# Hybrid encoder on one core: the filters' loads on ScalarE's queue, c loaded onto every partition, the softplus in the first mixer

## The chip, the core and the metric

The kernel runs on one core of a Trainium2 chip. Its engines work from queues of their own and meet through semaphores: TensorE (PE, with its weight loads PEld), VectorE (DVE), ScalarE (ACT), GpSimd (POOL) and SyncE (SP). SP computes nothing; it issues DMA transfers, and ScalarE issues some too. The metric is the device time of one execution in microseconds; lower is better. The time before is the median of three runs.

## The reference

A two-layer encoder on 256 tokens of width 2048. Each layer is modulated by a vector c, and its mixer has four groups (a gated linear recurrence, attention, a Hyena long convolution with learned filters, an mLSTM), followed by a SwiGLU. What matters here, cut down:

```python
c_act = silu(c)
for l in range(2):
    mod = c_act @ ada_w[l] + ada_b[l]            # 6 x 2048 numbers for each layer
    sh1, sc1, g1, sh2, sc2, g2 = split(mod, 6)
    h = rmsnorm(x, norm_mix_g[l]) * (1 + sc1) + sh1
    proj = h @ w_in[l] + b_in[l]
    y = concat(rglru(...), attention(...), hyena(...), mlstm(...))
    x = x + g1 * (y @ w_out[l])
    x = x + g2 * swiglu(rmsnorm(x, norm_ffn_g[l]) * (1 + sc2) + sh2)
return rmsnorm(x, final_g)

# Hyena's filters, they depend on weights alone
h = sin(sf * (feat @ w1 + b1)); h = sin(sf * (h @ w2 + b2)); h = h @ w3
h = h * exp(-t * abs(decay)); h = h / norm(h); spectrum = rfft(two_sided(h))
# rglru, in its gates
log_a = -8 * softplus(-lam) * r
```

## The kernel before, in words

The sequence lies along the free dimension: `x` is 16 tiles of 128 x 256, one for each 128 channels. Matrix products take weights as `raw` tiles of 128 x 1024 (512 KB), split by ScalarE into `hi` (L343) and by VectorE into `lo` (L344), and multiply them with `h` (L387 for the first eight `h` unsplit, L390 to L394 for the others).

`mod = c_act @ ada_w` runs on VectorE: each block of 128 outputs is two halves, each a transfer of 512 KB (`ada` or `ad`, L455 or by `load`, L313/L316) and one multiply with accumulation (L474) against `cb`, silu(c) on all partitions. Layer 0 needs 64 such halves before its last normalised `h` can be made, and the first seven fill all buffers (three `ada`, four `ad`). The others can be loaded only as VectorE frees a buffer.

The start of the program, `run`, does these things: `filters` (two small products and sines for each layer, the sine's argument reduced by six VectorE operations, L582 to L587); `ada_init` (loads c as one row, takes silu, spreads it to 128 partitions by four matmuls with a row of ones, L428, and copies them to `cb`, L430); the load and squares of `x` (ScalarE, summed on GpSimd, L523), which give `rb`, the reciprocal root mean square; `spectra` (L607 onwards: `third` loads the filters' last weights `w3`, `dft` the five transform tiles; decay `dec` L647, filter values L651, `he` L653/L654, transforms L675, results written to memory by ScalarE's queue, L693), in which a loop calls `early`, which does two halves of `mod` a turn and makes the `h` they allow; then `softplus` (two ScalarE functions and 22 VectorE operations of 128 x 16 or 128 x 8).

The order in which the code is written is not the order on the engines. The program is built by a scheduler (`schedule_with_timeline_sim`) that lists each engine's instructions by its own estimate of time; on the chip each engine then takes them strictly in that order. All transfers take turns at eight completion semaphores, DMAHW0 to DMAHW7, whichever queue issues them; a transfer waits until the one that last held its semaphore has landed, so no more than eight are under way. Names in the trace: `w` is a tile of `w3` or of the filters' weights, `m` a bank of PSUM, `z` and `n` the sine's argument, `sx`, `sz`, `ss` and `lam` the softplus.

Of the kernel before, what the change touches and what calls it, by code (L numbers as in the profile page):

```python
# [13 lines left out]
AF = mybir.ActivationFunctionType  # L14
# [4 lines left out]
P = 128  # L19
# [229 lines left out]
class Net:  # L249
# [170 lines left out]
    def ada_init(self, order):  # L420
        nc = self.nc
        self.cb = self.cp.tile([P, D], F32, name="cb")
        row = self.cb[0:1, :]
        nc.sync.dma_start(row, self.d["c"])
        nc.scalar.activation(row, row, AF.Silu)
        ps = [self.bank("cb") for _ in range(4)]
        for i in range(4):
            nc.tensor.matmul(ps[i], self.misc[0:1, 0:1].to_broadcast([1, P]), row[:, i * 512:(i + 1) * 512], start=True, stop=True)  # L428
        for i in range(4):
            nc.scalar.activation(self.cb[:, i * 512:(i + 1) * 512], ps[i], AF.Copy)  # L430
        self.mod = [self.cp.tile([P, 96], F32, name=f"mod{l}") for l in range(DEPTH)]
        self.acc = [self.cp.tile([P, 96, 2], F32, name=f"acc{l}") for l in range(DEPTH)]

        self.gain = {(l, j): self.cp.tile([P, 16], F32, name=f"gain{l}{j}") for l in range(DEPTH) for j in (1, 4)}
        self.ada_items = [(l, b, h) for l, b in order for h in range(2)]
        self.ada_at = self.ada_got = 0
        self.ada_left = 0.0
        self.ada_tiles = {}
# [127 lines left out]
    def dft(self):  # L566
        k = []
        for i in range(5):
            t = self.slot("dft")
            self.load(t, self.d["k_dft"][:, i])  # L570
            k.append(t)
        return k
# [19 lines left out]
    def filters(self):  # L592
# [3 lines left out]
        nc.sync.dma_start(ft[:17, :], d["k_feat"])  # L596
        w = self.cp.tile([64, DEPTH, P], F32, name="hw")
        nc.sync.dma_start(w, d["hy_w"])
# [8 lines left out]
    def spectra(self, h):  # L607

        nc = self.nc
        w3 = self.third(0)  # L610
        self.kept_dft = dft = self.dft()
# [10 lines left out]
    def third(self, l):  # L622

        w3 = [self.slot("w3") for _ in range(4)]
        for q in range(4):
            self.nc.sync.dma_start(w3[q][:68, :], self.d["hy_w3"][l, q])
# [497 lines left out]
    def mixer(self, l, h):  # L1124
# [4 lines left out]
        for hf in range(2):  # L1129
# [4 lines left out]
            yc += self.hyena(l, hf, pv, dft, spec, self.rs[l])  # L1134
        px = self.proj(l, h, 12, 2)
# [83 lines left out]
    def run(self, out):  # L1219
        nc, d = self.nc, self.d  # L1220
        order = [(0, j * 16 + k) for k in range(16) for j in (1, 0)]
        order += [(l, j * 16 + k) for l in range(DEPTH) for j in ((1, 0) if l else ()) + (2, 4, 3, 5) for k in range(16)]
        h2 = self.filters()
        self.ada_init(order)
# [13 lines left out]
        self.softplus()  # L1238
# [27 lines left out]
```

## Time and profile before

| | us |
|---|---|
| median of three runs | 2565.73 |
| lowest and highest | 2561.16, 2567.45 |
| the profiled execution | 2563.17 |
| its span, first to last instruction | 2561.4 |

Around the span lie 1.8 us. Read the busy shares of the engines first, then the same shares by slices, then stretches of the start, and in them what each engine waits for. In a timeline row the first number is the start in us, the second the length of the merged instructions, then engine, line, operation, names, shapes and count; in square brackets how long the engine sat idle before, and what ended that. A q behind the engine (SPq, ACTq) marks its queue, where a transfer is issued.

### The profile page before, as it was taken

The page shows a single profiled execution, that of the slowest core. Times are in us where ns is not written, and L with a number is a line of the kernel's source. Part 1 is how long each engine was busy: PE and PEld are TensorE (multiplying, and loading weights), DVE is VectorE, ACT ScalarE, POOL GpSimd, SP SyncE. Part 2 cuts the span into 40 slices and gives each one's busy share as a digit, 9 for nine tenths or more (in the row PEclk, how much of TensorE's full clock was granted, in tenths as well). Part 3 has the DMA queues.
Part 4 walks back from the last instruction along what each step waited for, and adds up shares of the span by engine and source line. Part 5 has one row for each costly group of instructions (what it writes and reads, how often), then busy time and mean ns, then how long its engine had stood idle before and what let it go on. Part 6 is the DMA issues. An engine that isn't in the chain of part 4 may idle for free. (4 is left out here: it accounts for less than half of the span.)

```text
span 2561.4 us, 38913 instructions
## 1 busy us (share of the span) xinstructions
PE 2470.3 (96%) x14962; PEld 2164.6 (85%) x14962; DVE 1839.4 (72%) x2862; ACT 1160.4 (45%) x1788; POOL 151.6 (6%) x142
## 2 busy tenths in 40 slices
PE   6879999999999999999998998999999999999998
PEld 2459988898888888888888998979888888888887
DVE  6877667689777777877787768777755555555555
ACT  4423344544544444444444455554444344434443
POOL 2101110021000000000010101002000000000001
PEclk9999999999999999999999999999999999999999
DMA  7887787688888888888887767658655655665554
GB/s 269 318 320 257 269 279 257 203 316 286 294 286 287 294 288 292 284 297 290 281 289 258 250 220 242 221 166 281 228 194 185 189 192 189 184 188 192 188 179 132
DMA packets 180719, 629.63 MB, mean 246 GB/s; under 512 B 20162, under 2 KB 20371, under 8 KB 180531
## 3 DMA queue, kind: packets, MB, share of 16 engines
q1 hardware_dynamic: 130996, 453.05, 53.9%
q10 hardware_dynamic: 49536, 174.09, 19.3%
q8 instruction: 117, 1.92, 0.3%
q14 instruction: 70, 0.57, 0.1%
HBM read 618.67 MB, written 8.39 MB: 245 GB/s over the span
## 5 line engine op out<-in xcount | busy, mean ns | idle before, releaser
L344 DVE TENSOR_TENSOR lo<-raw,hi 128x1024 fp32r<-128x1024 f32 (+2 forms) x737 | 891.8, 1211 | 471.8 <-ACT hi L343 463.4
L343 ACT ACTIVATE hi<-raw 128x1024 fp32r<-128x1024 f32 (+2 forms) x737 | 765.9, 1041 | 943.9 <-PE a L390 404.9
L394 PE MATMUL a<-h,lo 128*128 128x256 f32 x3848 | 1070.1, 284 | 5.7 <-DVE lo L344 5.7
L390 PE MATMUL a<-h,hi 128*128 128x512 f32 x2624 | 909.6, 396 | 0.0
L394 PEld LDWEIGHTS a<-h,lo 128*128 128x128 f32 x3848 | 735.2, 191 | 21.9 <-DVE lo L344 6.3
L390 PEld LDWEIGHTS a<-h,hi 128*128 128x128 f32 x2624 | 483.7, 188 | 107.4
L390 PE MATMUL a<-g,hi 128*128 128x512 f32 x1352 | 463.0, 396 | 0.0
L474 DVE SCALAR_TENSOR_TENSOR ada<-ada,cb 128x1024 f32<-128x1024 f32 x342 | 426.6, 1250 | 36.7 <-DMA ada<-in_ada 36.3
L392 PE MATMUL a<-h,hi 128*128 128x256 f32 x1224 | 359.9, 297 | 17.4 <-ACT h L558 12.3
L394 PE MATMUL a<-g,lo 128*128 128x256 f32 x1408 | 368.9, 279 | 0.0
L393 PE MATMUL a<-h,hi 128*128 128x256 f32 x1224 | 359.2, 294 | 7.3 <-DVE h L560 7.3
L390 PEld LDWEIGHTS a<-g,hi 128*128 128x128 f32 x1352 | 243.0, 188 | 47.8
L394 PEld LDWEIGHTS a<-g,lo 128*128 128x128 f32 x1408 | 265.6, 189 | 13.2
L392 PEld LDWEIGHTS a<-h,hi 128*128 128x128 f32 x1224 | 239.8, 197 | 24.6 <-ACT h L558 14.5
L393 PEld LDWEIGHTS a<-h,hi 128*128 128x128 f32 x1224 | 241.1, 197 | 12.7 <-DVE h L560 8.4
L523 POOL TENSOR_TENSOR sq<-sq,sq 128x256 f32<-128x256 f32 x65 | 75.5, 1161 | 1654.5 <-issue 1365.1
L387 PE MATMUL a<-h,raw 128*128 128x256 f32 x688 | 165.4, 393 | 3.8 <-DMA raw<-in_w_in 3.2
L387 PEld LDWEIGHTS a<-h,raw 128*128 128x128 f32 x688 | 132.2, 197 | 32.6 <-issue 8.6
L1160 DVE SCALAR_TENSOR_TENSOR x<-a,mod,x 128x256 f32<-128x256 f32 x228 | 100.2, 476 | 28.0 <-PE a L394 28.0
L1177 ACT ACTIVATE s<-a 128x256 f32<-128x256 f32 x82 | 31.5, 384 | 119.1 <-PE a L394 119.1
L1178 DVE TENSOR_TENSOR s<-s,a 128x256 f32<-128x256 f32 x82 | 34.4, 420 | 35.9 <-ACT s L1177 35.9
L558 ACT ACTIVATE h<-h,mod 128x256 fp32r<-128x256 f32 (+1 forms) x64 | 29.5, 501 | 62.8 <-DVE h L554 36.4
(268 smaller groups left out, 2170.5 us busy)
## 6 DMA issues: line engine op xcount, KB each, us to landing
raw<-in_w SPq DMA_DIRECT2D x496, 512.0 KB, 4.6
ada<-in_ada ACTq DMA_DIRECT2D x320, 512.0 KB, 5.4
raw<-in_w_in SPq DMA_DIRECT2D x168, 512.0 KB, 5.3
raw<-in_w_out SPq DMA_DIRECT2D x64, 512.0 KB, 5.6
ad<-in_ada SPq DMA_DIRECT2D x42, 512.0 KB, 7.2
raw<-in_w SPq DMA_DIRECT2D x32, 384.0 KB, 3.7
ada<-in_ada SPq DMA_DIRECT2D x22, 512.0 KB, 6.1
spectra<-sl ACTq DMA_DIRECT2D x24, 256.0 KB, 7.4
```

Of the source, the lines that this page charges most:

```text
L343: self.hi_at = self.nc.scalar.activation(hi[:, :n], t[:, :n], AF.Copy).ins
L344: self.lo_at = self.nc.vector.tensor_tensor(lo[:, :n], t[:, :n], hi[:, :n].bitcast(F32), ALU.subtract).ins
L387: mm(o, hi[:, c], a[:, :T], start=first and b == 0, stop=last, skip_group_check=True)
L390: mm(ps[b], hi[:, c], a, start=first, stop=False, skip_group_check=True)
L392: mm(o, hi[:, c], a[:, :T], start=first and b == 0, stop=False, skip_group_check=True)
L393: mm(o, hi[:, c], a[:, T:], start=False, stop=False, skip_group_check=True)
L394: mm(o, lo[:, c], a[:, :T], start=False, stop=last, skip_group_check=True)
L474: nc.vector.scalar_tensor_tensor(t, t, 1.0, self.cb[:, h * 1024:(h + 1) * 1024], ALU.mult, ALU.mult, accum_out=acc[:, b, h:h + 1])
L523: nc.gpsimd.tensor_tensor(self.sq, self.sq, t, ALU.add)
L1160: i = self.nc.vector.scalar_tensor_tensor(self.x[k], o, g, self.x[k], ALU.mult, ALU.add)
L1177: nc.scalar.activation(s, ps[0][:, T:], AF.Copy)
L1178: nc.vector.tensor_tensor(s, s, ps[0][:, :T], ALU.add)
```

## The change

Four things are changed. c is loaded by one transfer onto all 128 partitions and silu taken there; the row, the four matmuls and the four copies go. The filters' features `feat`, their weights `hw`, the first layer's four `w3` tiles and the five transform tiles `dft` are loaded by ScalarE's queue, and `w3` and `dft` are asked for right after `filters` in place of inside `spectra`. `ada_init` stands ahead of `filters`. `softplus` is written in the first mixer, behind the two Hyena halves.

```diff
     def ada_init(self, order):
         self.cb = self.cp.tile([P, D], F32, name="cb")
-        row = self.cb[0:1, :]
-        nc.sync.dma_start(row, self.d["c"])
-        nc.scalar.activation(row, row, AF.Silu)
-        ps = [self.bank("cb") for _ in range(4)]
-        for i in range(4):
-            nc.tensor.matmul(ps[i], self.misc[0:1, 0:1].to_broadcast([1, P]), row[:, i * 512:(i + 1) * 512], start=True, stop=True)
-        for i in range(4):
-            nc.scalar.activation(self.cb[:, i * 512:(i + 1) * 512], ps[i], AF.Copy)
+        nc.sync.dma_start(self.cb, self.d["c"].to_broadcast([P, D]))
+        nc.scalar.activation(self.cb, self.cb, AF.Silu)
...
-    def dft(self):
+    def dft(self, first=False):
...
-            self.load(t, self.d["k_dft"][:, i])
+            if first:
+                self.nc.scalar.dma_start(t, self.d["k_dft"][:, i])
+            else:
+                self.load(t, self.d["k_dft"][:, i])
...
-        nc.sync.dma_start(ft[:17, :], d["k_feat"])
+        nc.scalar.dma_start(ft[:17, :], d["k_feat"])
-        nc.sync.dma_start(w, d["hy_w"])
+        nc.scalar.dma_start(w, d["hy_w"])
...
-        w3 = self.third(0)
-        self.kept_dft = dft = self.dft()
+        w3 = self.w3
+        self.kept_dft = dft = self.first_dft
...
-            self.nc.sync.dma_start(w3[q][:68, :], self.d["hy_w3"][l, q])
+            (self.nc.sync if l else self.nc.scalar).dma_start(w3[q][:68, :], self.d["hy_w3"][l, q])
...
+        if l == 0:
+            self.softplus()
         px = self.proj(l, h, 12, 2)
...
+        self.ada_init(order)
         h2 = self.filters()
-        self.ada_init(order)
+        self.w3 = self.third(0)
+        self.first_dft = self.dft(True)
...
-        self.softplus()
```

What the scheduler makes of it. SP's queue before, from the last of the first seven halves of `mod` to the eighth, `ada_246` (in brackets the semaphores an instruction waits for):

```order
L313 DMA ada_220<-in_ada 128x1024 [waits DMAHW0_49]
L626 DMA w_59_269<-in_hy_w 68x512 [waits DMAHW1_49]
...
L313 DMA dft_278<-in_k_dft 128x512 [waits DMAHW5_49]
...
L313 DMA dft_286<-in_k_dft 128x512 [waits DMAHW1_49]
L626 DMA w_118_429<-in_hy_w 68x512 [waits DMAHW2_49]
...
L328 DMA raw_455<-in_w_in 128x1024 [waits DMAHW6_49]
...
L328 DMA raw_465<-in_w_in 128x1024 [waits DMAHW3_49]
L313 DMA ada_246<-in_ada 128x1024 [waits DMAHW4_49,DVE_49]
```

The same place now; the eighth half is `ada_253`:

```order
L313 DMA ada_227<-in_ada 128x1024 [waits DMAHW1_49]
L623 DMA w_114_417<-in_hy_w 68x512 [waits DMAHW2_49]
...
L623 DMA w_117_420<-in_hy_w 68x512 [waits DMAHW5_49]
L328 DMA raw_443<-in_w_in 128x1024 [waits DMAHW6_49]
...
L328 DMA raw_453<-in_w_in 128x1024 [waits DMAHW3_49]
L313 DMA ada_253<-in_ada 128x1024 [waits DMAHW4_49,DVE_49]
```

Nineteen transfers stood between the two halves, of which ten are left; the four first `w` and the five `dft` have gone to ScalarE's queue.

ScalarE's queue at the start of the program, before:

```order
L1017 ACT_TABLE_LOAD
L1017 ACTIVATE sx<-lam 128x16 [waits DVE_49]
L1018 ACTIVATE sx<-sx 128x16 [waits Activation_49]
L425 ACT_TABLE_LOAD
L425 ACTIVATE cb<-cb 1x2048 [waits DMAHW5_49]
L517 ACTIVATE sq_162<-x 128x256 [waits DMAHW6_49]
```

and now:

```order
L593 DMA feat_93<-in_k_feat 17x256
...
L623 DMA w_21_148<-in_hy_w 68x512 [waits DMAHW3_49]
L625 ACT_TABLE_LOAD
L625 ACTIVATE w_18_145<-w_18_145 4x512 [waits DMAHW5_49]
...
L424 ACT_TABLE_LOAD
L424 ACTIVATE cb<-cb 128x2048 [waits DMAHW6_49]
L586 ACTIVATE sin_107<-z_99 64x256 [waits DVE_49]
...
L1015 ACT_TABLE_LOAD
L1015 ACTIVATE sx<-sx 128x16 [waits Activation_49]
...
L586 ACT_TABLE_LOAD [waits DVE_49]
```

Six issues stand first, and the first sine and the squares stand behind two waits for transfers; the softplus's second function (L1015) is still in the first rows, between the squares, and brings a change of table with it and one back. Four table loads stand here, of two before.

VectorE's queue up to the eighth half, before (`ada_207` is the first half):

```order
L587 TENSOR_SCALAR z_124<-z_124 64x256 [waits DVE_49]
L474 SCALAR_TENSOR_TENSOR ada_207,acc_151<-ada_207,cb 128x1024 [waits DMAHW2_49,Activation_49]
...
L654 TENSOR_TENSOR he_335<-m_333,he_335 128x512 [waits PE_49]
L474 SCALAR_TENSOR_TENSOR ada_246,acc_151<-ada_246,cb 128x1024 [waits DMAHW4_49]
L474 SCALAR_TENSOR_TENSOR ad_225,acc_151<-ad_225,cb 128x1024 [waits DMAHW5_49]
L481 SCALAR_TENSOR_TENSOR mod_149<-acc_151,par 128x1 [waits DVE_49]
L654 TENSOR_TENSOR he_366<-m_364,he_366 128x512 [waits PE_49,Activation_49]
```

and now (`ada_214` is the first half):

```order
L1017 TENSOR_SCALAR sz<-sx 128x16 [waits Activation_49]
L584 TENSOR_SCALAR z_123<-z_123 64x256 [waits DVE_49]
...
L468 SCALAR_TENSOR_TENSOR ada_214,acc_87<-ada_214,cb 128x1024 [waits DMAHW0_49]
L1023 TENSOR_TENSOR ss<-ss,sz_1730 128x16 [waits DVE_49]
...
L651 TENSOR_TENSOR he_323<-m_321,he_323 128x512 [waits PE_49]
L468 SCALAR_TENSOR_TENSOR ada_253,acc_87<-ada_253,cb 128x1024 [waits DMAHW4_49]
...
L468 SCALAR_TENSOR_TENSOR ad_256,acc_87<-ad_256,cb 128x1024 [waits DMAHW0_49]
L651 TENSOR_TENSOR he_354<-m_352,he_354 128x512 [waits PE_49,Activation_49]
```

The softplus starts later and reaches in between the first halves; five halves of `mod` (`ada_253`, `ad_232`, `ad_235`, `ada_264`, `ad_256`) now stand between `he_323` and `he_354`, where two stood between `he_335` and `he_366`.

## Rows read from the trace of the kernel before

**Rows 1.** The page: busy time of PE, and PE in 40 slices (tenths).

```profile
PE 2470.3 (96%) x14962; PEld 2164.6 (85%) x14962; DVE 1839.4 (72%) x2862; ACT 1160.4 (45%) x1788; POOL 151.6 (6%) x142
...
PE   6879999999999999999998998999999999999998
```

**Rows 2.** Stretches: us, busy us of PE, PEld, DVE, ACT, POOL, clock, DMA share, GB/s.

```profile
0.00:21.25 21.25, 10.31 (x16) 3.79 (x16) 16.59 (x52) 12.34 (x26) 10.26 (x17) 1.00 0.87 312
21.25:29.34 8.09, 3.61 (x14) 2.63 (x12) 8.09 (x16) 2.11 (x4) 0.00 (x0) 1.00 0.59 165
29.34:49.81 20.47, 16.21 (x23) 6.80 (x24) 4.24 (x13) 6.50 (x10) 1.60 (x2) 1.00 0.97 324
49.81:191.60 141.79, 120.39 (x417) 73.20 (x416) 116.87 (x232) 50.74 (x103) 19.23 (x12) 0.94 0.84 306
...
200.00:300.00 100.00, 100.00 (x592) 91.92 (x591) 74.43 (x124) 29.50 (x54) 13.60 (x16) 1.00 0.82 279
```

**Rows 3.** Timeline of VectorE, 21 to 58 us.

```profile
21.25 1.21 DVE L474 SCALAR_TENSOR_TENSOR ada<-ada,cb 128x1024 f32<-128x1024 f32 x1
...
31.18 0.87 DVE L554 SCALAR_TENSOR_TENSOR h<-x,gain,rb 128x256 f32<-128x256 f32 x2 [1.16 <-PE rb L542]
...
47.49 0.69 DVE L654 TENSOR_TENSOR he<-m,he 128x512 f32<-128x512 f32 x1 [8.20 <-PE m L651]
...
49.81 1.46 DVE L474 SCALAR_TENSOR_TENSOR ada<-ada,cb 128x1024 f32<-128x1024 f32 x1
...
57.28 0.69 DVE L654 TENSOR_TENSOR he<-m,he 128x512 f32<-128x512 f32 x1 [3.54 <-PE m L651]
```

**Rows 4.** Timeline of TensorE, three places.

```profile
34.71 3.78 PE L651 MATMUL m<-w,sin 64*128 64x512 f32 x4
...
41.70 3.75 PE L387 MATMUL a<-h,raw 128*128 128x256 f32 x8 [3.21 <-DMA raw<-in_w_in]
...
192.85 1.01 PE L392 MATMUL a<-h,hi 128*128 128x256 f32 x3 [0.82 <-ACT h L558]
```

**Rows 5.** Timeline of SP's queue, 17 to 39 us.

```profile
17.15 6.83 SPq L313 DMA_DIRECT2D dft<-in_k_dft  x5
25.32 3.91 SPq L626 DMA_DIRECT2D w<-in_hy_w  x4
29.66 6.92 SPq L328 DMA_DIRECT2D raw<-in_w_in  x6
38.49 0.33 SPq L313 DMA_DIRECT2D ada<-in_ada  x1
```

**Rows 6.** Timeline of ScalarE, three places in the first 35 us.

```profile
4.36 1.28 ACT L425 ACT_TABLE_LOAD   x1
5.65 1.91 ACT L425 ACTIVATE cb<-cb 1x2048 f32<-1x2048 f32 x1
...
34.09 0.62 ACT L628 ACTIVATE w<-w 4x512 f32<-4x512 f32 x1 [9.80 <-DMA w<-in_hy_w]
```

**Rows 7.** Timeline of all engines: softplus, the sum of squares, its matmuls.

```profile
6.66 0.15 DVE L1026 TENSOR_TENSOR ss<-ss,sz 128x16 f32<-128x16 f32 x1
...
9.06 10.16 POOL L523 TENSOR_TENSOR sq<-sq,sq 128x256 f32<-128x256 f32 x12 [8.62 <-ACT sq L521]
...
12.59 0.68 DVE L1026 TENSOR_TENSOR ss<-ss,sz 128x16 f32<-128x16 f32 x1
...
22.14 2.72 PE L532 MATMUL ss<-misc,sq 128*128 128x1 f32 x12
```

**Rows 8.** DMA view, 0 to 60 us in 40 slices: busy tenths, GB/s.

```profile
DMA  0738999999999998632259999999999998387620
GB/s 0 224 82 195 339 407 388 415 415 418 423 374 421 285 254 221 194 119 90 98 162 300 257 283 262 266 310 410 418 399 423 401 407 330 120 311 251 243 96 11
```

**Rows 9.** Waits of VectorE, 49 to 192 us: us in total, times, longest.

```profile
DVE r L505 <- ACT a L504: 7.9, 3, 4.6
...
DVE lo L344 <- ACT hi L343: 5.1, 1, 5.1
```

## The prediction

> **What bounds the kernel now.** Read the busy shares first. TensorE is busy for 96% of the span, and in the slices only the first four stand clearly under 9 [rows 1]. The stretches say the same: from 200 to 300 us TensorE is busy for 100.00 of 100 us, while in the first 21.25 us it works 10.31 and VectorE 16.59, from 21.25 to 29.34 VectorE works 8.09 of 8.09, and from 29.34 to 49.81 VectorE works only 4.24 of 20.47 [rows 2]. So a change at the start can bring something only by letting TensorE reach its steady state earlier. That point stands in TensorE's timeline: at 192.85 it waits a last 0.82 us for an `h` [rows 4]. Behind it the order of the instructions is the same before and after, so a shift of that point should reach the end one for one.
>
> The last of layer 0's first normalised `h` needs all 64 halves of `mod`, 1.21 us each [rows 3], so 77 us of VectorE at least. The first starts at 21.25; seven of them fill the time to 29.34 (8.09 us). The eighth starts only at 49.81 [rows 3]. In between VectorE waits, for 8.20 us at one place, for the products of L651 that `he` needs. TensorE is what it waits for there: two pairs of L651 take 3.78 us for four instructions, and ahead of the eight unsplit products at 41.70 TensorE itself stood for 3.21 us waiting for a `raw` to land [rows 4]. SP's queue tells why that `raw` was late: five `dft` were being issued from 17.15 for 6.83 us, four `w` from 25.32 for 3.91, six `raw` from 29.66 for 6.92, and the eighth half of `mod` was asked for at 38.49 [rows 5]. A transfer is held until one of eight semaphores is free, so the queue moves at the rate of landing. Last, the bytes: the first 20 us run at 410 to 420 GB/s in their busy slices, but around 25 to 28 us only at 98, with two or three tenths of the DMA engines' time [rows 8]; the whole stretch 21.25 to 29.34 has a share of 0.59 and 165 GB/s [rows 2]. There is room in it.
>
> From 49.81 to 191.60 VectorE is busy 116.87 of 141.79 and TensorE 120.39 [rows 2]: both are nearly full and hand waits to each other, so a gain at 49.81 is likely but not certain to arrive at 192.85.
>
> **The change part by part.** *c on all partitions.* Gone are a transfer of 8 KB, four matmuls and four copies. New is a transfer of 1.05 MB, 1.04 MB more; at the 410 GB/s of the busy slices [rows 8] that is 2.6 us of DMA time, at 98 GB/s it would be 10.7. Silu on 1x2048 took 1.91 us [rows 6]; ScalarE's time goes by the elements of a partition, and I take 1.91 again. Before, `cb` was not what the first half waited for: VectorE worked 16.59 of 21.25 [rows 2] and had sines and softplus ahead of it.
>
> *ScalarE's start.* Before, its first table load was at 4.36 and Silu at 5.65 [rows 6]. Now six issues, an Abs of 0.62 [rows 6], two more issues and a second table load stand ahead of Silu: SP paid 6.92 for six issues with waits, 3.91 for four, and 0.33 for one that had nothing ahead [rows 5], so with free semaphores some 0.4 each. 8 x 0.4 + 2 x 1.28 + 0.62 = 6.4, with the two waits for landings some 8 us; Silu to about 10 if c has landed. The first sine comes at about 10.4 and the squares from 11.5. GpSimd's sums (12 in 10.16 us, 0.85 each [rows 7]) and a thirteenth then end at about 23.7; TensorE's sum over partitions began at 22.14 before [rows 7]. Before, this path had slack for some of that: `h` at 31.18 had waited only 1.16 us for `rb` [rows 3]. I take **+1.0 us** for the first `h`; bounds 0 and +3.
>
> *The softplus.* It is written later, but the order has its second function (L1015) and most of VectorE's part still at the start; its table change costs 1.28 and one back 1.28 [rows 6]. The clamp of the second sine's argument now stands behind L1017, so the first half of `mod` starts at about 23 (bounds 21 and 24.5). While GpSimd worked, one small softplus operation took 0.68 in place of 0.15 [rows 7]; 22 of them are 3.3 to 15 us, which were ahead of the first half and now lie partly between the first seven. Since VectorE waits 8.20 us right after [rows 3], this is covered, and costs nothing as long as seven halves end before about 36.
>
> *The queue.* SP has ten transfers in place of nineteen ahead of the eighth half. The six `raw` can be asked for some 9 transfers earlier, and land at about 29 to 34, ahead of their use. The 3.21 us go. Of the eight unsplit products (3.75 [rows 4]) only four stand ahead of the fourth `he` in the new order: 1.9 us less. The eighth half then starts at 49.81 - 3.21 - 1.9 + 1.0 = 45.7: **-4.1 us** (bounds 44.5 and 47; 49.8 if TensorE finds another wait). Its own data, asked for ten us earlier than 38.49, do not bind.
>
> *The fifth `he`.* It stood at 57.28 after a wait of 3.54 for TensorE [rows 3], with two halves of `mod` in front of it; now five. Three more halves are 3 x 1.21 = 3.6 us of work that must be done anyway: **-3.5 us** (bounds 0, if their data are not there, and -3.6).
>
> *A wait behind.* In 49 to 192 us VectorE waited once 5.1 us for a `hi`, and 7.9 in three times for a softmax's scale [rows 9]. The first stands behind a ScalarE that had no free buffer; in the new order this `lo` stands further back, behind a later `h`. Whether all of it is won the trace of before can't say; between 0 and -5.1 I take the middle, **-2.5 us**. The 7.9 stay.
>
> Sum: -4.1 - 3.5 - 2.5 = -10.1. On the profiled execution, 2563.17, that is 2553.1. The median lies 2.6 above that execution, so **2555.7, say 2556**. With the lower bounds of the gains (-2.8 + 0 + 0) it would be 2563, with the upper (-5.3 - 3.6 - 5.1 = -14.0) 2552; a gain that grows in the hand-over of the two full engines could bring it to 2548.
>
> **Page and row.** The four `w` have 68 rows, and while they alone moved the share was two to three tenths at some 98 GB/s [rows 8]. By the Trainium skill ("DMA: Bandwidth & Descriptors", "Why a DMA increments its semaphore by 16 and not by 1") a transfer is spread over the largest number of engines, up to 16, that divides its outer dimension, here four; the trace's quarter agrees. By that page the four `w` ahead of c would keep these four engines busy for an estimated 5.4 us (4 x 34 KB each at a sixteenth of 410 GB/s) and c, which uses all, would land that much later. The sum above doesn't need it.
>
> **The rivals.** *Nothing gained (0.28).* The bytes are the same plus 1.04 MB, and the moved transfers run on the same DMA engines: the queue waits for landings, not for its turn to issue. Then what SP no longer issues is only landed by others ahead of the same `raw`, and `raw` arrives as late as before; or it arrives, and the chain L651, `he`, L651 on TensorE and VectorE, which is unchanged, sets the eighth half anyway and the covered waits come back at the next step. Price: -2.6 (some covered) to +2.6 (c's bytes), 2563 to 2568, **2565**. For it: the busy slices at 410 to 420 GB/s before 20 us [rows 8], and a share of 0.97 from 29.34 to 49.81 [rows 2]. Against it: the 98 GB/s and the share of 0.59 just before [rows 2, 8], in which SP was held by four narrow transfers. The Trainium skill ("DMA: Bandwidth & Descriptors", "Issuing engines are not separate DMA queues") speaks for this rival: it says that starting transfers from several engines saves only the time to issue. What speaks against the rule here is that SP's order, with waits in it, held transfers back while engines stood idle [rows 5, 8].
>
> *ScalarE held at the start (0.10).* ScalarE takes its queue in order. Abs waits for a `w`, Silu for c, and behind them stand both sines, all squares, and so `rb` and the first `h`. Before, the same Abs stood 9.80 us, to 34.09, for a `w` that SP had asked for at 25.32 [rows 5, 6], 8.8 us at most for 139 KB. If that comes back here, with c at 98 GB/s (10.7 us) behind it, Silu ends at 18 to 28 rather than 10. Each us of it moves sines, squares and the first `h` alike. From a delay of 10 us on (the sum of the gains) nothing is won; from 18 on it is slower by over 0.3%. Two such waits, 8.8 + 10.7, less the slack of 1.2, make 2565.7 - 10.1 + 18.3 = **2574**. Against it: transfers onto 128 partitions ran at 410 (that all read one row of 8 KB, as c's do, no row shows), and only four `w` and two small transfers are ahead on this queue.
>
> *The change doesn't do what it says.* The softplus keeps its place in part (two table loads more). It is in the sum already, as ScalarE's 2.56 us.
>
> **How the numbers follow.** A measurement of this kernel can tell about 0.3% from no change, 7.7 us: faster means under 2558.0, slower over 2573.4. The forecast has 0.62, from 2548 to 2560, of which 0.53 lies under 2558. The rival of no gain has 0.28, of which 0.03 under 2558 and the rest within. ScalarE held has 0.10, 0.08 of it over 2573.4. Together faster 0.56, same 0.36, slower 0.08. The range 2548 to 2568 leaves out most of the last rival and a little below, under 2 in 10.
>
> **What would show it.** Right: the first half of `mod` at about 23 us, the first `h` at about 32, no wait of TensorE for a `raw` ahead of the unsplit products, the eighth half at about 45.7, no wait of VectorE at the fifth `he`, no 5.1 us at a `lo`, and TensorE's last wait for an `h` at about 183 in place of 192.85. Wrong at its first step: Silu ending well after 10 us or the first `h` after 35. Wrong at the second: the eighth half at 49 or later though the `raw` are there. Wrong at the last: the eighth half early, but TensorE's last wait still at 190 or later, which would mean that the two full engines ate the gain; or a point at 183 and an end that has not moved by ten.

## The result and the profile after

| | before | after |
|---|---|---|
| median, us | 2564.54 (8 runs) | 2580.60 (8 runs) |
| lowest and highest | 2561.16, 2567.45 | 2571.71, 2590.65 |
| the profiled execution, its span | 2563.17, 2561.4 | 2574.87, 2573.1 |

The change made the kernel slower: ratio 1.0059, 95% interval 1.0047 to 1.0070. A second measurement, beside later runs, gave 1.0049 (1.0034 to 1.0064). The prediction had 2556, within 2548 to 2568, and gave slower 0.08. The time went at the start. The page of after, with TensorE's busy time and its 40 slices, shows it: the first three slices are 3, 8 and 8 tenths where [rows 1] have 6, 8 and 7.

```profile
span 2573.1 us, 38888 instructions
...
PE 2463.0 (96%) x14954; PEld 2161.0 (84%) x14954; DVE 1840.8 (72%) x2862; ACT 1160.9 (45%) x1786; POOL 153.9 (6%) x142
...
PE   3889999999999999999998998999999999999998
```

TensorE's busy time fell by 7.3 us against [rows 1], and the span grew by 11.7 us: TensorE stood idle for 110.1 us in place of 91.1.

Three stretches of after: up to the first half of `mod`, from there to the eighth half, and from there to the last `h` of layer 0's first normalisation (columns as in [rows 2]):

```profile
0.00:37.99 37.99, 4.16 (x8) 1.30 (x8) 13.76 (x39) 14.33 (x28) 8.90 (x16) 1.00 0.86 270
37.99:62.23 24.24, 17.18 (x31) 8.08 (x32) 15.18 (x39) 6.94 (x11) 4.95 (x4) 1.00 0.79 259
62.23:199.96 137.73, 119.67 (x418) 71.36 (x417) 116.30 (x231) 50.87 (x103) 19.38 (x12) 0.91 0.88 303
```

Before, the first half stood at 21.25 [rows 3]; up to 37.99 VectorE now works only 13.76 us and TensorE 4.16. ScalarE's timeline says why. This is its queue from the four `w` to the first square of `x`:

```profile
1.85 3.56 ACTq L623 DMA_DIRECT2D w<-in_hy_w  x4
5.44 1.28 ACT L625 ACT_TABLE_LOAD   x1 [5.44 <-DMA w<-in_hy_w]
11.71 0.62 ACT L625 ACTIVATE w<-w 4x512 f32<-4x512 f32 x1 [4.98 <-DMA w<-in_hy_w]
11.71 5.24 ACTq L565 DMA_DIRECT2D dft<-in_k_dft  x2
16.98 1.28 ACT L424 ACT_TABLE_LOAD   x1 [4.65 <-DMA w<-in_hy_w]
18.27 1.91 ACT L424 ACTIVATE cb<-cb 128x2048 f32<-128x2048 f32 x1
20.09 0.40 ACT L586 ACTIVATE sin<-z 64x256 f32<-64x256 f32 x1
20.91 6.36 ACTq L565 DMA_DIRECT2D dft<-in_k_dft  x3
27.32 0.42 ACT L511 ACTIVATE sq<-x 128x256 f32<-128x256 f32 x1 [6.83 <-DMA dft<-in_k_dft]
```

The Abs waits 4.98 us for a `w` to land. Then come two issues of `dft` that take 5.24 us, since one stands in the queue until its semaphore is free, and three more that take 6.36; behind the one and the other ScalarE was idle for 4.65 and 6.83 us. Together 16.5 us of waiting stand ahead of the first square, which came at 8.26 before and comes at 27.32 now. VectorE takes its own queue in order too. Its timeline at the places that [rows 3] show of before, and the first two waits:

```profile
21.69 0.53 DVE L579 TENSOR_SCALAR z<-m,par 64x256 f32<-64x256 f32 x1 [10.61 <-PE m L600]
...
29.10 0.17 DVE L1026 TENSOR_SCALAR lam<-lam 128x16 f32<-128x16 f32 x1 [6.23 <-ACT sx L1014]
...
37.99 1.75 DVE L468 SCALAR_TENSOR_TENSOR ada<-ada,cb 128x1024 f32<-128x1024 f32 x1
...
48.57 0.48 DVE L548 SCALAR_TENSOR_TENSOR h<-x,gain,rb 128x256 f32<-128x256 f32 x1 [1.42 <-PE rb L536]
...
62.23 1.46 DVE L468 SCALAR_TENSOR_TENSOR ada<-ada,cb 128x1024 f32<-128x1024 f32 x1
...
71.41 0.69 DVE L651 TENSOR_TENSOR he<-m,he 128x512 f32<-128x512 f32 x1 [0.89 <-PE m L648]
...
199.96 0.48 DVE L548 SCALAR_TENSOR_TENSOR h<-x,gain,rb 128x256 f32<-128x256 f32 x1
```

The seven first halves stand behind rows that wait for the held sines (10.61 us, by way of TensorE's second product) and the held softplus function (6.23). SP is held as well. In its timeline the last halves of the seven are asked for at 27.78 and 28.62; before, the seventh was asked for at 10.77, ahead of the `dft` and `w` of [rows 5]:

```profile
19.19 0.33 SPq L313 DMA_DIRECT2D ada<-in_ada  x1
27.78 0.80 SPq L313 DMA_DIRECT2D ad<-in_ada  x2
28.62 0.43 SPq L313 DMA_DIRECT2D ada<-in_ada  x1
```

and its view of waits, up to 60 us, names a transfer of the other queue:

```profile
SPq L313 <- DMA dft<-in_k_dft: 8.2, 1, 8.2
```

One queue's next half waits for the semaphore of a `dft` that ScalarE had not yet been free to ask for. Eight semaphores taken in turn by two queues tie the one to what holds the other.

### The profile page after: what moved, and what is told of

The parts are those of the page before. It is cut to its first block, busy times and chain, and to the rows that moved or that the text cites. A ratio compares the mean times of both kernels' runs of the same rounds, so it can differ in the third digit from the quotient of the medians.

```text
span 2573.1 us, 38888 instructions
## 1 busy us (share of the span) xinstructions
PE 2463.0 (96%) x14954; PEld 2161.0 (84%) x14954; DVE 1840.8 (72%) x2862; ACT 1160.9 (45%) x1786; POOL 153.9 (6%) x142
## 5 line engine op out<-in xcount | busy, mean ns | idle before, releaser
L392 PEld LDWEIGHTS a<-h,hi 128*128 128x128 f32 x1224 | 240.8, 198 | 20.2 <-ACT h L552 11.5
```

The source lines that it names most:

```text
L392: mm(o, hi[:, c], a[:, :T], start=first and b == 0, stop=False, skip_group_check=True)
```

## The experiments

All times in this table are of one profiled execution each: start of the first square, first half of `mod`, first `h`, eighth half, last `h`, and the span. The ratio is of all runs against the kernel before on the same chip, with its interval. (The profiled execution of "`dft` back, 64 rows" is the slowest of its ten.) For every version the scheduler lists the engines' instructions anew, so an event also moves because it is listed elsewhere: the eighth half stands behind four `he` on VectorE before and in the changed kernel, behind three to none of them in most others.

| run | square | first half | first `h` | eighth | last `h` | span | ratio (95%) |
|---|---|---|---|---|---|---|---|
| before | 8.26 | 21.25 | 31.18 | 49.81 | 191.77 | 2561.4 | 1 |
| changed | 27.32 | 37.99 | 48.57 | 62.23 | 199.96 | 2573.1 | 1.0059 (1.0047-1.0070) |
| changed, again | 26.92 | 37.59 | 48.17 | 61.83 | 199.86 | 2575.4 | 1.0049 (1.0034-1.0064) |
| c alone | 10.16 | 18.77 | 33.52 | 46.31 | 187.68 | 2559.6 | 1.0001 (0.9992-1.0011) |
| queue alone | 26.21 | 34.33 | 47.73 | 55.74 | 197.41 | 2569.1 | 1.0020 (1.0010-1.0031) |
| loads on SP | 21.01 | 26.69 | 43.23 | 52.68 | 192.43 | 2563.6 | 1.0012 (1.0002-1.0021) |
| `dft` back | 17.46 | 26.50 | 37.39 | 50.63 | 190.48 | 2558.2 | 1.0001 (0.9992-1.0011) |
| `w` back | 18.11 | 26.76 | 39.23 | 52.28 | 192.13 | 2560.9 | 1.0010 (0.9999-1.0020) |
| `w` of 64 rows | 18.02 | 25.53 | 39.52 | 47.53 | 199.16 | 2570.1 | 1.0023 (1.0012-1.0034) |
| `dft` behind | 18.15 | 27.19 | 38.09 | 46.10 | 199.64 | 2567.8 | 1.0038 (1.0023-1.0053) |
| behind, 64 rows | 13.03 | 22.81 | 34.48 | 42.49 | 190.27 | 2561.7 | 1.0000 (0.9989-1.0012) |
| `dft` back, 64 rows | 13.36 | 23.14 | 34.81 | 42.83 | 191.20 | 2567.8 | 1.0002 (0.9992-1.0013) |
| c alone, 64 rows | 10.80 | 18.33 | 34.76 | 41.07 | 194.24 | 2564.5 | 1.0029 (1.0018-1.0040) |
| before, 64 rows | 9.05 | 21.52 | 31.46 | 36.16 | 186.13 | 2560.5 | 1.0003 (0.9993-1.0013) |
| 14 copies | 23.33 | 17.32 | 41.20 | 46.83 | 186.71 | 2559.6 | 0.9986 (0.9977-0.9995) |
| 14 copies, again | 21.28 | 15.26 | 40.07 | 46.05 | 188.23 | 2563.0 | 0.9990 (0.9981-0.9999) |
| 28 copies | 37.56 | 15.38 | 53.35 | 49.30 | 192.18 | 2567.3 | 1.0027 (1.0014-1.0040) |
| 28 copies, sines too | 25.00 | 15.55 | 51.89 | 48.68 | 189.45 | 2562.4 | 0.9991 (0.9981-1.0001) |
| halves first | 26.96 | 21.09 | 45.82 | 54.50 | 193.64 | 2569.5 | 1.0037 (1.0024-1.0050) |
| c alone, halves first | 10.38 | 15.51 | 32.63 | 46.62 | 195.25 | 2572.6 | 1.0055 (1.0039-1.0071) |

**The parts apart.** The theory after the two traces, Q in the expectations: transfers that wait in ScalarE's queue hold sines and squares. C: c's megabyte does it. B: the early bytes and their order do it, on any queue. The softplus needs no run: with it moved into the mixer or back, in either kernel, the lists of instructions are the same row by row on all five engines. That part of the change does nothing.

c alone, the kernel before with

```diff
-        row = self.cb[0:1, :]
...
+        nc.sync.dma_start(self.cb, self.d["c"].to_broadcast([P, D]))
+        nc.scalar.activation(self.cb, self.cb, AF.Silu)
```

> The kernel before with one part of the change alone: c loaded by one transfer onto all partitions, silu taken there; all other loads stay on SP's queue and in their old place. Theory Q (the waits of the transfers that now stand in ScalarE's queue hold squares and sines): no such transfers here, so the first half of mod starts at 19 to 24 us, the first h at 30 to 34, time 2558 to 2567, that is 0 to -0.3% of before. Rival C (c's 1 MB onto 128 partitions lands late and holds ScalarE at Silu): first h at 40 or later, time 2574 or more. Rival B (bytes and order: the w and dft ahead of x and of the halves, whichever queue asks): as before, 2562 to 2567, +2.6 us at most for c's bytes.

No change (1.0001), as Q and B have it. The first `h` came at 33.52, not at 40 or later: c's bytes alone cost nothing, so C falls as an explanation by itself.

Queue alone, the kernel before with ScalarE's issues, `w` and `dft` behind `filters`:

```diff
         h2 = self.filters()
+        self.w3 = self.third(0)
+        self.first_dft = self.dft(True)
```

> The kernel before with the other part alone: features, filter weights, the first four w and the five dft loaded early by ScalarE's queue; c stays one row with matmuls and copies, the softplus stays. Theory Q: like the changed kernel, first h at 44 to 52 us, 2572 to 2582. Rival C: no megabyte of c here, so 2552 to 2560. Rival B: like the changed kernel less c's 2.6 us, 2570 to 2579; this run does not tell Q from B.

Slower by 0.20%. It is the queue, but short of the expected 2572: 2568.92. With c it is 0.5 to 0.6%; the two together cost more than each. Without c's megabyte the Abs started at 7.68 in place of 11.71, and the issues of `dft` moved up with it, two from 11.71 to 7.69 and three from 20.91 to 15.56.

Loads on SP, the changed kernel with the same early order but one queue:

```diff
-                self.nc.scalar.dma_start(t, self.d["k_dft"][:, i])
+                self.nc.sync.dma_start(t, self.d["k_dft"][:, i])
```

and likewise for `feat`, `hw` and `w`.

> The changed kernel with one thing undone: features, filter weights, w and dft are asked for at the same early place in the program, but by SP's queue; c onto all partitions stays. Theory Q: ScalarE's queue holds no transfer, so squares start when x lands, which is after 11 small transfers: first square at 13 to 18 us, first h at 33 to 38, the eighth half at 47 to 53, time 2556 to 2568. Rival B (order and bytes, not the queue): like the changed kernel, first h at 45 or later, 2572 to 2582. Rival C: the same as B's, 2572 or more.

With the queue alone edited, 1.0059 (or 1.0049) becomes 1.0012. The time is Q's, not B's, though the events came later than Q had them (first square at 21.01, first `h` at 43.23). But the order on the engines is not the same: both functions of the softplus stand ahead of Silu here, and VectorE does all of the softplus ahead of the second sines' arguments. So the loss goes with the queue and the order that comes with it; this run does not part the two. ScalarE now waits for `x`, and VectorE for its first half, since both stand behind eleven small transfers. ScalarE's and VectorE's timelines:

```profile
21.01 0.42 ACT L511 ACTIVATE sq<-x 128x256 f32<-128x256 f32 x1 [6.51 <-DMA x<-in_xT]
...
26.69 1.74 DVE L468 SCALAR_TENSOR_TENSOR ada<-ada,cb 128x1024 f32<-128x1024 f32 x1 [8.01 <-DMA ada<-in_ada]
```

`dft` back on SP and inside `spectra`; then, in another kernel, the `w` back and the `dft` early:

```diff
-        self.first_dft = self.dft(True)
...
-        self.kept_dft = dft = self.first_dft
+        self.kept_dft = dft = self.dft()
```

> The changed kernel with the five dft alone taken back: asked for inside spectra by SP's queue as before; features, filter weights and the four w stay early on ScalarE's queue. Theory Q: the dft waits of 5.24 and 6.36 us in ScalarE's queue go, the Abs wait for a w (5 us, to 11.7) stays: first square at 14 to 18 us, first h at 34 to 39, time 2556 to 2567. If it is the w alone that hold it (Q's other half, the Abs): first h at 44 or later, 2570 or more. Rival C: 2572 or more. Rival B: 2566 to 2575, for half of the early bytes are gone.

```diff
-        self.w3 = self.third(0)
...
-        w3 = self.w3
+        w3 = self.third(0)
```

> The changed kernel with the four first w alone taken back: asked for inside spectra by SP's queue, Abs with them; the five dft stay early on ScalarE's queue. With the run in which the dft alone were taken back this makes a square of four. If the dft cost what they cost only because narrow w stand ahead of them and keep semaphores (the two together make the delay): no wait of over 2 us in ScalarE's queue, first square at 10 to 14 us, last h of layer 0 at 186 to 193, time 2558 to 2566, no slower than before. If five transfers of 256 KB in ScalarE's queue are enough by themselves: first square at 18 or later, last h at 195 or later, 2568 or more. If c and the queue together are enough: the same, 2568 or more.

Either one taken back takes the loss away, or most of it: 1.0001 and 1.0010. With c alone, which also has `feat` and `hw` on SP's queue, this is nearly a square of four: neither 1.0001, `w` 1.0001, `dft` 1.0010, both 1.0049 to 1.0059. The loss is made by the two together, each time with the order that the scheduler makes of it. The reading "no wait of over 2 us" without the `w` was wrong all the same: five issues of 256 KB took ScalarE's queue for 8.34 us, and with four table loads of 1.28 us behind them the first square came at 18.11.

```profile
1.85 8.34 ACTq L565 DMA_DIRECT2D dft<-in_k_dft  x5
10.22 1.28 ACT L1014 ACT_TABLE_LOAD   x1 [10.22 <-DMA dft<-in_k_dft]
...
18.11 0.40 ACT L511 ACTIVATE sq<-x 128x256 f32<-128x256 f32 x1
```

**The queue and narrow transfers.** The changed kernel was run again beside these three.

> The changed kernel itself once more, on the chip of the three that follow, so that they are compared with it under the same conditions. The runs so far put the end 2508 to 2513 us behind the start of the eighth half of mod. Theory Q (transfers that wait in ScalarE's queue): first square at 25 us or later, first half of mod at 35 to 42, eighth half at 58 to 68, time 2571 to 2591, ratio 1.003 to 1.008. That single transfer waits and not a fixed cost make it would show as a spread of 10 us or more between its runs, with the same order on every engine.

It came out as the first time, though with 6 us between its four runs where 10 or more were expected (the first eight had 19).

```diff
-            (self.nc.sync if l else self.nc.scalar).dma_start(w3[q][:68, :], self.d["hy_w3"][l, q])
+            e = self.nc.sync if l else self.nc.scalar
+            if q == 0:
+                e.dma_start(w3[q][64:68, :], self.d["hy_w3"][l, q, 64:68])
+            e.dma_start(w3[q][:64, :], self.d["hy_w3"][l, q, :64])
```

> The changed kernel, with each w loaded as 64 rows (and the 4 rows of the decay, of the first w alone, by a transfer of their own) in place of 68 rows. Everything stays on ScalarE's queue in front of sines and squares. If narrow transfers are the cause (68 rows move at some 98 GB/s, so Abs waits to 11.71 us and semaphores stay taken): w lands some 4 to 6 us earlier, first square at 15 to 20 us, eighth half at 50 to 55, time 2561 to 2568. If it is the dft's waits for a semaphore whatever the w do: first square at 23 to 28, time 2570 to 2582.

The first square comes 9 us earlier. The Abs, listed behind Silu and the first sine here, has nothing left to wait for, and the five issues of `dft` take 2.70 us in all, where they took 11.60:

```profile
10.01 0.37 ACTq L565 DMA_DIRECT2D dft<-in_k_dft  x1
...
11.97 0.36 ACTq L565 DMA_DIRECT2D dft<-in_k_dft  x1
12.24 0.62 ACT L628 ACTIVATE w<-w 4x512 f32<-4x512 f32 x1
13.86 1.64 ACTq L565 DMA_DIRECT2D dft<-in_k_dft  x2
...
17.64 0.33 ACTq L565 DMA_DIRECT2D dft<-in_k_dft  x1
18.02 0.42 ACT L511 ACTIVATE sq<-x 128x256 f32<-128x256 f32 x1 [2.06 <-DMA dft<-in_k_dft]
```

The Trainium skill ("DMA: Bandwidth & Descriptors", "Why a DMA increments its semaphore by 16 and not by 1") says that a transfer uses the largest number of DMA engines, up to 16, that divides its outer dimension: four for 68 rows, 16 for 64. The traces agree: around the second four `w`, where [rows 8] fall to 90 to 119 GB/s, the kernel before with 64 rows (further down) has no slice under 217 from 25.5 to 33 us. Half of the loss goes with the narrow `w` (1.0049 to 1.0023), but the eighth half at 47.53 did not bring the expected 2561 to 2568: the median is 2569.36, and the last `h` stayed at 199.16.

```diff
+        with self.tc.issue_after(self.last_sq):
+            self.first_dft = self.dft(True)
```

> The changed kernel with one thing changed: the five dft stay on ScalarE's queue, but are asked for behind the last square. Nothing else is moved by hand. Theory Q: the dft hold nobody, only Abs's wait for a w is left; first square at 14 to 18 us, first h at 34 to 38, eighth half at 44 to 51, time 2555 to 2563, not slower than before. If ScalarE's queue as such or the bytes of c are to blame: 2570 or more.

This expectation missed: 1.0038, and 2573.81 lies where ScalarE's queue as such would put it. The squares were free (18.15), and the five issues, now behind the last square, stand ahead of the next thing in ScalarE's queue, the first `h`. The first row is VectorE's:

```profile
38.09 0.48 DVE L548 SCALAR_TENSOR_TENSOR h<-x,gain,rb 128x256 f32<-128x256 f32 x1
...
30.96 9.93 ACTq L565 DMA_DIRECT2D dft<-in_k_dft  x5
40.94 0.51 ACT L552 ACTIVATE h<-h,mod 128x256 f32<-128x256 f32 x1 [13.26 <-DMA dft<-in_k_dft]
```

Of the 13.26 us that ScalarE sat idle the issues cost this `h` only the last 2.4, from VectorE's end at 38.57 on. What else makes the 0.38% is not shown. With both edits together:

> Both together: the dft on ScalarE's queue behind the last square, and each w as 64 rows. Theory Q with narrow w as its second part: Abs no longer waits for long, first square at 10 to 14 us, first h at 30 to 34, eighth half at 42 to 47, time 2552 to 2560, faster than before by 0.1 to 0.4%. If the eighth half is then bound by its own data or by TensorE's products (as in the run with c alone, where it stood 3.05 us for its data), 2558 to 2564, no change.

the first half stood at 22.81, the eighth at 42.49, 7 us ahead of before, and the time was that of before (1.0000). The events came as the first of its two readings had them, the time as the second; what the second gave as the reason, an eighth half that waits, was not seen.

**Does an early eighth half pay at all?** Three runs on it, each with the `w` of 64 rows as above: c alone, the changed kernel with the `dft` back, and the kernel before.

> The kernel before with c on all partitions, all loads on SP's queue in their old place, and each w as 64 rows in place of 68 (the decay's 4 rows apart). If SP's queue gets through faster because the w no longer move at 98 GB/s (3.9 to 4.1 us for each four, twice): the raw and the eighth half are asked for 3 to 6 us earlier than with c alone, last h at 181 to 187 us, time 2552 to 2559, faster than both kernels. If the stretch behind the eighth half takes it back (as in the runs with the dft behind the squares, where the eighth half was 3.7 us earlier than before and the last h 7.9 later): 2559 to 2568.

> The changed kernel with the dft back on SP's queue inside spectra, and each w as 64 rows, early on ScalarE's queue. The run with the dft back and w of 68 rows had Abs wait to 11.49, the first square at 17.46, the first half at 26.5. If narrow w are what held Abs: first square at 12 to 15 us, first half at 21 to 25, last h at 185 to 191, time 2556 to 2564. If something else holds the start: first half at 26 or later.

> The kernel before with one thing changed: each w as 64 rows. Narrow w as a cost of SP's queue: raw at TensorE's first unsplit product no longer late (3.21 us before), eighth half at 44 to 48 in place of 49.81, last h at 185 to 190, time 2555 to 2562. If the w were hidden: no change, 2560 to 2566.

It does not show in the time. The plainest is the last: VectorE's eighth half 13.65 us earlier, the last `h` 5.64 earlier, and no change (1.0003). With c on all partitions as well it is even slower than before, 1.0029, beyond both readings, though the eighth half is 8.74 us early. The changed kernel with the `dft` back had its first half at 23.14 and 1.0002, as its first reading had it. Three rows of VectorE's timeline, and the stretch between the first and the last of them in the view of stretches, of before with 64 rows:

```profile
36.16 1.23 DVE L474 SCALAR_TENSOR_TENSOR ada<-ada,cb 128x1024 f32<-128x1024 f32 x1 [3.82 <-DMA ada<-in_ada]
...
44.57 0.69 DVE L656 TENSOR_TENSOR he<-m,he 128x512 f32<-128x512 f32 x1
...
186.13 0.48 DVE L554 SCALAR_TENSOR_TENSOR h<-x,gain,rb 128x256 f32<-128x256 f32 x1
```

```profile
36.16:186.13 149.97, 129.10 (x426) 76.22 (x425) 117.83 (x234) 50.75 (x106) 20.38 (x12) 0.89 0.86 317
```

The fourth `he` of the kernel before, and its stretch from the eighth half to the last `h`:

```profile
49.20 0.69 DVE L654 TENSOR_TENSOR he<-m,he 128x512 f32<-128x512 f32 x1 [1.02 <-PE m L651]
```

```profile
49.81:191.77 141.96, 120.56 (x418) 73.33 (x416) 117.04 (x233) 50.74 (x103) 19.23 (x12) 0.94 0.84 306
```

Most of the 13.65 us is order. Before, the eighth half is listed behind the first four `he`; with 64 rows it is listed ahead of all four. The fourth `he`, the same work in both, came 4.63 us earlier (44.57 in place of 49.20). That is what the chain gained, and the last `h` shows it. So the two stretches do not hold the same work, and their 8.0 us of difference say little: the one with 64 rows holds eight more unsplit products, eight more of L653 (L651 before) and eight fewer split products. By the groups of instructions these are some 7 of the 8.5 us by which TensorE is busy longer. The granted clock of the stretch is 0.89 in place of 0.94 (a mean of parts at 2.4 and at 1.2 GHz); what it costs, no run isolated. Of the 5.64 us at the last `h`, 0.9 us is left at the end of the profiled span: behind it TensorE is busy 2323.78 us (x14504) in place of 2319.57 (x14496). Why the rest goes is open.

**A hold alone.** Is a held ScalarE enough? Copies of 128x512 that nobody reads, put on ScalarE ahead of the squares, in the kernel with c alone:

```diff
+        ps = self.bank("hold")
+        for _ in range(28):
+            held = nc.scalar.activation(ps, self.misc[:, 0:1].to_broadcast([P, 512]), AF.Copy).ins
+        with self.tc.issue_after(held):
             for k in range(KT):
                 self.square(k)
```

> The run with c alone, with 14 copies of 128x512 put on ScalarE ahead of the squares (some 8 us); no transfer on ScalarE's queue, nothing else changed by hand. Theory Q (a hold of ScalarE at the start delays the squares, rb and the first h, and with them the end): first square at 18 to 20 us in place of 10.2, first h at 38 to 42, last h of layer 0 at 188 to 193, time 2561 to 2567: part of it falls into VectorE's wait ahead of the eighth half. Rival T (transfers and shared semaphores make the delay): no change against c alone, last h at 186 to 189, 2559 to 2565.

> The same with 28 copies (some 16 us, as long as ScalarE's waits in the changed kernel). Theory Q: first square at 26 to 29 us, first h at 46 to 50, last h at 195 to 202, time 2569 to 2578, ratio 1.002 to 1.006. Rival T: last h at 186 to 192, 2559 to 2566.

With the sines behind the copies as well, and c asked for first:

```diff
+        with self.tc.issue_after(self.held):
             nc.scalar.activation(h[q], z[q], AF.Sin)
```

> The 28 copies ahead of both squares and all four sines, c asked for first; again no transfer on ScalarE's queue. Since the copies were known when the order was made, VectorE takes seven halves ahead of the second sine's argument, where the changed kernel takes sines first. Theory Q, with the order as its second part: first half at 14 to 20 us, first h at 47 to 52, last h at 192 to 199, time 2565 to 2575. If the hold costs the same whatever the order: last h at 198 to 203, 2571 to 2578. Rival T: 2559 to 2566.

The answers differ. With the sines held too, the first `h` at 51.89 is later than in the changed kernel, and the time is 0.9991 of before, as the rival T had it:

```profile
15.55 1.23 DVE L468 SCALAR_TENSOR_TENSOR ada<-ada,cb 128x1024 f32<-128x1024 f32 x1 [2.10 <-DMA ada<-in_ada]
...
51.89 0.87 DVE L548 SCALAR_TENSOR_TENSOR h<-x,gain,rb 128x256 f32<-128x256 f32 x2 [1.65 <-PE rb L536]
```

28 copies ahead of the squares alone held them to 37.56, further than meant, since two Abs came to stand among the copies; that cost 0.27%, and 2570.86 lies in Q's range, the last `h` at 192.18 not. So a first `h` as late as the changed kernel's need not cost anything by itself, but squares held 10 us longer do cost. What the copies do not do is hold VectorE's first halves (15.55 here, 37.99 there) or SP's queue. With 14 copies the first `h` came at 41.20 and the kernel was even 0.14% faster than before; the run was repeated:

> The run with c alone and 14 copies ahead of the squares once more; it had 0.9986 of before, 0.9977 to 0.9995. If that was the order that the copies made (first half at 17.32 in place of 18.77, GpSimd's sums out of the way of VectorE's arguments): again 0.997 to 0.9995. If it was chance: 0.9995 to 1.001.

Again 0.9990. It is the one version whose interval lies under 1, both times, by 0.1%, less than the 0.3% of the prediction's bound. Why idle copies help where c alone does nothing is open; the order on VectorE differs too.

**The halves first.** The changed kernel with its queues, but VectorE's seven halves ahead of the second sines, the softplus and `rb`; then the same move in the kernel with c alone:

```diff
-        self.ada(4)
+        self.ada(7)
+        self.seven = self.half
+        h2 = self.layer(h2, 64, 64, "hb2")
...
+        with self.tc.issue_after(self.half):
             i = nc.vector.tensor_scalar(v, ps[:, :2], 1.0 / D, EPS, ALU.mult, ALU.add)
```

> The changed kernel with ScalarE's queue and all transfers as they are, but VectorE's seven first halves placed ahead of all that waits for the held ScalarE (second sines' arguments, most of the softplus, rb's scaling). First square at 26 to 28 us as before. Theory D (VectorE's halves queue behind work that waits for ScalarE): first half at 20 to 22 us in place of 38, seventh at 30 to 37, last h of layer 0 at 188 to 194, time 2560 to 2568, ratio 0.999 to 1.002. If the transfers are the cause (halves land late, semaphores shared with ScalarE's queue): seventh half at 37 or later, last h at 196 or later, 2570 to 2582.

> The run with c alone (all transfers on SP's queue in their old place), with the same move of the seven halves. First half at 12 to 14 us in place of 18.77, the seventh at 20 to 24. If an earlier start of the halves is worth time: eighth half at 38 to 44, last h at 180 to 186, 2551 to 2559. If the stretch behind the eighth half takes it back, as in the runs with w of 64 rows: last h at 185 to 190, 2558 to 2565.

The first half came at 21.09 as expected, and the last `h` 6.3 us earlier than in the changed kernel, but the time only came down to 1.0037: 2572.58 lies where the transfers as the cause would put it. The second run says why this does not decide: the move by itself, without any changed queue, costs 0.54% (1.0055 against 1.0001), more than either of its readings. In both the second sines come behind the first `h` and change ScalarE's table back and forth (four loads of 1.28 us between 46.96 and 58.29 in the first); whether that is the cost is not shown. So an order alone can cost about as much as the whole change. How much of the change's loss goes by the late halves, how much by SP's late transfers, and how much by the order that came with the queue stays open.

## Why the prediction was wrong

**What bounds the kernel.** Right in the main: the time was lost at the start. But a shift does not reach the end one for one, and the order behind that point is not the same before and after: TensorE's list differs up to some 270 us. The prediction's own mark, TensorE's last wait for an `h`, moved from 192.85 to 197.86, by 5.0 us, the last `h` by 8.2 and the end by 11.7:

```profile
197.86 0.62 PE L392 MATMUL a<-h,hi 128*128 128x256 f32 x3 [1.75 <-ACT h L552]
```

In the twenty profiled executions the span minus the start of the last `h` lies between 2367.7 and 2377.4 us, so a shift of that point reaches the end to within some 5 us either way. The steps ahead of it failed.

**ScalarE's start** is the step that failed first and most. It took "six issues, an Abs, two more issues and a second table load" as some 8 us, with an issue at 0.4 "with free semaphores", and Silu to about 10, the squares from 11.5. Measured: Silu ended at 20.18, the squares began at 27.32. The semaphores were not free. The price that it lacked stood in [rows 5]: five `dft` took SP's queue 6.83 us, four `w` 3.91. The step named such prices beside its 0.4, but read them as what SP would be rid of and did not charge them to the queue that took them over. The last three issues of `dft`, between first sine and squares, it left out altogether (6.36 us). The term +1.0 for the first `h` measured +17.4 (31.18 to 48.57).

**The rival "ScalarE held"** named the right queue and had 0.10. Its 2574 lies close to the profiled 2574.87 (the median is 2580.60), but by other waits, so that part is luck. It looked for the hold in the Abs and in c. The Abs was there (4.98 us); Silu did not wait for c, and the larger part, 11.5 us, were the `dft` issues. The rule of the Trainium skill that was weighed for the other rival ("DMA: Bandwidth & Descriptors", "Issuing engines are not separate DMA queues": several issuing engines save only the time to issue) fits what was seen. There was little to save, and by "loads on SP" the second queue, with the order that it brings, cost 0.4 to 0.5%.

**The first half** was put at 23, bounds 21 and 24.5; it came at 37.99. That the clamp stands behind a softplus row was seen. What was missed is that the wait for it carries ScalarE's delay, and that all halves queue behind it.

**The queue** came as forecast, and more: TensorE's wait for a `raw` is gone, and from the end of the seventh half to the eighth it took 10.89 us (51.34 to 62.23) in place of 20.47. With a start 22 us later the term of -4.1 became +12.4.

**The fifth `he`** waited 0.89 in place of 3.54: -2.65 of the -3.5. **The wait for a `hi`**, 5.1 us [rows 9], shrank to 1.6 at most; but the softmax's scale, which "stays" at 7.9, rose to 14.1. From the eighth half to the last `h`, after took 137.73 us, before 141.96: -4.2, where the two terms had -6.0. The sum is near, but in part by luck, since a wait that was to stay grew by 6.2.

**That a gain at the eighth half arrives** was called likely. "Before, 64 rows" puts that in doubt: there the wait for a `raw` is gone as the queue term had it, the fourth `he` comes 4.63 us earlier and the last `h` 5.64, and the time is 1.0003. So even with the start as forecast, -10.1 may not have come through; no run had such a gain to show it.

**The softplus** was in the sum by its two table loads. The move does nothing; the two loads come with the rest of the change, which puts its second function between squares and sines. "Queue alone", where the softplus is not moved, has it there as well, with a table load at 28.88 and one back at 31.50.

## What to carry to other kernels

In these runs a transfer cost the engine that issued it what the transfer waited for, not what a free issue takes. Before moving loads to a computing engine's queue, read how long that group of issues held its old queue, and list what stands behind it on the new one. And before an event is compared between two versions, see whether the same work stands ahead of it in both lists: here the eighth half came 13.65 us earlier, mainly since it was listed ahead of four other rows, while the chain gained 4.6 us and the end stayed.

## What the runs showed of the hardware

Two issuing queues that take turns at the same eight semaphores hold each other: SP stood 8.2 us for a `dft` that ScalarE had not asked for yet. An issue took 0.33 to 0.53 us where its semaphore was free; three `dft` took 6.36 us and five 8.34 to 9.93 where not. Four `w` of 68 rows kept the Abs waiting to 11.71 us, and the five `dft` behind them took 11.60 us to issue; with the `w` as 64 rows and four apart, the Abs at 12.24 had nothing left to wait for, and the five issues took 2.70. Small changes at the start (the halves first, `w` of 64 rows with c alone) moved the whole time by 0.3 to 0.5%, and no single step was found in them that costs so much.
